# Turned tiles of w_up begun and landed by a table of steps, in place, with a second place for the tile turned last

## The chip, the cores and the metric

The kernel runs on one core of a Trainium2 chip. The metric is the time of one execution on the device in microseconds (us); lower is better. Five engines work side by side, each through its own queue in order: TensorE (PE in the profile, with its weight loads as PEld), VectorE (DVE), ScalarE (ACT), GpSimd (POOL) and SyncE (SP). Here POOL and SP do little but issue transfers (DMAs).

## The reference

One decoder layer for 256 tokens of width 2048, all in float32: a mixer (a state-space group and an attention group side by side) and then a feed-forward part. The change touches the feed-forward part only:

```python
def squared_relu_mlp(u, w_up, w_down):
    hdn = jax.nn.relu(jnp.einsum('bsd,df->bsf', u, w_up))
    return jnp.einsum('bsf,fd->bsd', hdn * hdn, w_down)

h = h + rmsnorm(squared_relu_mlp(rmsnorm(h, norm_mlp_pre), w_up, w_down), norm_mlp_post)
```

`w_up` is 2048 x 8192 and `w_down` 8192 x 2048.

## The kernel before

**Products.** TensorE multiplies numbers of reduced precision, so each float32 operand is split into a high and a low part: `split` (L145) writes `hi` on ACT (L148) and `lo = src - hi` on DVE (L149). A product is three matmuls, `hi*hi`, `hi*lo` and `lo*hi`. Weights come from DRAM in pieces of 256 rows by 512 columns (`raw`, or other buffers that are free at that time), issued on SP; each is split into one of five `hi`/`lo` pairs.

**Units.** A unit (`unit`, L488) makes two neighbouring blocks of 512 output columns for both halves of the tokens (`t` = 0, 1). It goes through `order`, a list of pieces of 256 rows of the weight. At each *step* of it (the loop from L494; steps are counted from 0) it multiplies either in the plain way (`row_tiles`, 24 matmuls with two pieces) or by Strassen's seven products in place of eight (`seven`, 21 matmuls), which needs sums of weights on DVE (L263) and one piece that GpSimd has added up in DRAM. The sevens go into four banks of their own (`more`). After the last of them `combine_new` (L459) brings these banks together into four tiles in SBUF: L464 on ACT, L465 to L468 on DVE, in this order. The last pieces (`last`) are then multiplied plainly, and at each result `at_end` adds the combined part. The next unit uses `acc` and `more` with their places changed, so it begins to write a bank only when `combine_new` has read it.

A w_up unit has seven steps (sevens at steps 1, 3, 4 and 6) and one last piece. The stages after the mixer are: a first pair of w_up blocks made in another way; w_up units for blocks 2, 4 and 6 of the first half; two w_down units; w_up units for blocks 0, 2, 4 and 6 of the second half; two w_down units. The first w_down unit of each half has 14 steps.

**Turned tiles.** A w_up unit ends with four tiles of tokens by features (128 x 512): block 0 with `t` = 0 and 1, then block 1 with `t` = 0 and 1, here called the first to the fourth. They lie in `room["shared"]`: two in `hb`, two in `wpost`. Before w_down can use one, it must be squared, turned to features by tokens, and split. `up_end` (L1486) queues this as `turned` (L1495), a generator in two parts:

- *Begin* (`pump_beside`, L338): Relu with a scale (L1500), Square (L1501), a copy that sorts the upper and lower 16-bit words of the tile into one of two `halves` (L1502), and a transposing DMA on SP from `halves` back into the tile (L1503).
- *Land* (`land_beside`, L347): a copy that puts the words together into `junk` (L1506), and the split into `sh`/`sl` or the `att` tiles (L1508, recorded as L148 and L149).

The tiles of one unit are turned during the next one. A tile is begun at the head of each step from step 2 on. A tile is landed at the end of a step when the oldest one has seen more than two such ends. Before `combine_new`, `drain_beside` (L357) lands whatever is left, because `combine_new` writes the same four tiles. So the first tile is landed at the end of step 4, the second of step 5, and in a w_up unit the third and the fourth at the end of step 6, right before `combine_new`. `hp.tile(..., name="junk")` has one buffer.

**Order.** A planner puts the instructions of each engine in order ahead of time, by its own estimate of when each is ready. Instructions inside `tc.high_priority` (the splits of weights, `combine_new`, the sums at a unit's end) go first; the turned tiles have normal priority, and `tc.issue_after(newest["act"].ins)` keeps each part behind the last split of weights issued on ACT until then. Waits between engines follow from which tile is read and written: a write of a buffer waits for all reads of what was in it.

Of the kernel before, what the change touches and what calls it, by code (L numbers as in the profile page):

```python
# [10 lines left out]
F32 = mybir.dt.float32  # L11
F32R = mybir.dt.float32r
BF16 = mybir.dt.bfloat16
U16 = mybir.dt.uint16
AF = mybir.ActivationFunctionType
ALU = mybir.AluOpType

P = 128
# [21 lines left out]
NB = 512  # L40
# [14 lines left out]
V_SEVENS = (1, 3, 5, 6)  # L55
QK_SEVENS = (1, 3, 5, 6)
PAIRS_AHEAD = 4


def constants():  # L60
# [18 lines left out]
def hymba_layer(ctx: ExitStack, tc: tile.TileContext, x, norm_mix_pre, w_in, conv_w, conv_b, dt_bias, a_log,  # L79
                d_skip, ssm_norm_w, w_out, norm_mix_post, norm_mlp_pre, w_up, w_down, norm_mlp_post,  # L80
                consts, out):
    nc = tc.nc
# [31 lines left out]
    def part(k):  # L114
        if k < NK:
            return sh, sl, k
        i, r = divmod(k - NK, NK // 2)
        return (*att[i], r)
# [26 lines left out]
    def split(hi, lo, src, scale=None):  # L145

        if scale is None:
            return (nc.scalar.activation(hi, src, AF.Copy),  # L148
                    nc.vector.tensor_tensor(lo, src, hi.bitcast(F32), op=ALU.subtract))  # L149
        return (nc.scalar.activation(hi, src, AF.Copy, scale=scale),  # L150
                nc.vector.scalar_tensor_tensor(lo, src, scale, hi.bitcast(F32), op0=ALU.mult, op1=ALU.subtract))
# [27 lines left out]
    room = {}  # L179
# [13 lines left out]
    def beside_up(raws, turn, halves=None):  # L193

        room["sums"] = [v[:, k:k + KB] for k in range(0, NK // 2, KB) for v in att[1]]
        b = hp.tile([P, NT, NB], F32, name="hb")
        room["shared"] = [[b[:, t] for t in range(NT)],
                          [hp.tile([P, NB], F32, name="wpost", bufs=2) for _ in range(NT)]]
        a = hp.tile([P, 3 * KB, NB], F32, name="ha")
        in_a = [a[:, k:k + KB] for k in range(0, 3 * KB, KB)]  # L200
        halves = in_a.pop(0) if halves is None else halves
        room["halves"] = deque(halves[:, i].bitcast(U16) for i in range(KB))
        room["raw"], room["turn"], room["acts"], room["chain"] = [*raws, *in_a], turn, act_u, True
        room["of_halves"], room["of_a"] = halves, in_a
        sums_of.clear()
# [67 lines left out]
    def blocks_of(n):  # L273
        return n if isinstance(n, tuple) else (n * NB, (n + 1) * NB)
# [19 lines left out]
    paired = []  # L294
    places = [dram.tile([P, NB], F32, name=f"pair{i}") for i in range(PAIRS_AHEAD + 1)]

# [35 lines left out]
    def drain():  # L332
        while waiting:
            pump()

    beside, flying = deque(), deque()

    def pump_beside():  # L338

        if not beside:  # L340
            return
        work = beside.popleft()
        with tc.issue_after(newest["act"].ins):
            next(work)
        flying.append([work, 0])

    def land_beside(steps=2):  # L347

        for one in flying:
            one[1] += 1  # L350
        if flying and flying[0][1] > steps:
            with tc.issue_after(newest["act"].ins):
                next(flying.popleft()[0], None)
        if not (beside or flying) and "then" in room:
            room.pop("then")()

    def drain_beside():  # L357
        while beside or flying:
            pump_beside()
            land_beside(0)  # L360

    def row_tile(dst, t, parts, k0, acts, begin, end, cs=slice(0, NB)):

# [124 lines left out]
    def unit(src, n, order, last, acc, more, combine, lag=0, at_end=(None, None), first=True, ending=None,  # L488
             ready=None, halves=None):


        cols = blocks_of(n)
        sevens = [k for k, by_seven in order if by_seven]
        for i, (k, by_seven) in enumerate(order):  # L494
            if i >= 2:
                pump_beside()
            if i + 1 < len(order) and order[i + 1][1]:
                sums_of_acts(order[i + 1][0])
            if by_seven:
                if k == sevens[0]:  # L500
                    drain()
                    if ready:
                        ready()
                seven(src, *cols, k, acc, more, k == sevens[0], k == sevens[-1])
            else:
                for b in range(2):
                    row_tiles(src, cols[b], [k], acc[b::2], room["acts"], first and i == 0, False,
                              fetch=fetch_next)
            land_beside()
            if k == sevens[-1]:  # L510
                drain_beside()
                combine(more)
        for b in range(2):
            if b and ending:
                ended.append(ending(cols[b], last, acc))
            else:
                row_tiles(src, cols[b], last, acc[b::2], room["acts"], False, True, lag if b else 0, at_end[b],
                          fetch=fetch_last if b else fetch_next, halves=halves if b else None)
# [185 lines left out]
    def steps():  # L704
# [5 lines left out]
        with tc.high_priority(offset=AHEAD):  # L710
            for _ in range(PAIRS_AHEAD):
                next_pair()
# [614 lines left out]
    hp = ctx.enter_context(tc.tile_pool(name="hp", bufs=1, reuse_waits="tile"))  # L1327
# [167 lines left out]
    def turned(t, k, r):  # L1495
        room["halves"].rotate(1)
        halves = room["halves"][0]
        ts = slice(t * P, (t + 1) * P)
        words = r.bitcast(U16)
        nc.scalar.activation(r, r, AF.Relu, scale=rmlp[:, t:t + 1])  # L1500
        nc.scalar.activation(r, r, AF.Square)  # L1501
        nc.scalar.activation(halves.rearrange("p (h n) -> p h n", h=2), words.rearrange("p (n h) -> p h n", h=2), AF.Copy)  # L1502
        nc.sync.dma_start_transpose(words.rearrange("p (n s) -> p n s", s=P), halves)  # L1503
        yield
        whole = hp.tile([P, NB], F32, name="junk")
        nc.scalar.activation(whole.bitcast(U16).rearrange("p (n h) -> p h n", h=2), words.rearrange("p (h n) -> p h n", h=2), AF.Copy)  # L1506
        d_h, d_l, i = part(k)
        split(d_h[:, i:i + 4, ts], d_l[:, i:i + 4, ts], whole.rearrange("p (f s) -> p f s", f=4))  # L1508

    def onto_new_mw(more):  # L1510

# [14 lines left out]
    for hf in range(2):  # L1526
        if hf:
            beside_up([], 0)
        for fb in range(0 if hf else 2, 8, 2):
            unit(w_ups[hf], fb, orders[("up", hf), fb], (7,), acc, more,  # L1530
                 lambda x: combine_new(room["shared"], x), 0, (up_end(fb, 0), up_end(fb + 1, 1)))
            acc, more = more, acc
        if hf == 0:
            beside_down()
            unit(w_down, 0, orders[("down", 0), 0], (14, 15), acc, more,
                 lambda x: combine_new(in_mw(0), x), 0, (onto(0), onto(1)))
            room["raw"], room["turn"] = [new_mw(2)], 0
            room["sums"] += room["sums"][:4]
            unit(w_down, 2, orders[("down", 0), 2], (12, 14, 15), more, acc,
                 onto_new_mw, 0, (onto(2), onto(3)))  # L1540
# [65 lines left out]
```

## Time and profile before

| what | value |
|---|---|
| median of 3 runs | 1448.54 us (1445.23 to 1449.48) |
| the profiled execution | 1448.34 us |
| span of its trace | 1446.6 us |
| mean granted clock of TensorE | 0.999 of full speed |
| moved by DMA | 340.31 MB, mean 235 GB/s |

A view of waits lists who waited for what: total us, how many times, longest. A timeline row gives start, duration, engine, line, operation and the tiles as `written<-read`, with the idle time before it and what ended it in brackets. `L149` is line 149 of the kernel; a helper's line stands for all its callers, and the tile names tell them apart (`lo<-raw,hi` is a weight, `sl<-junk,sh` or `al<-junk,ah` a turned tile). The busy time of TensorE counts pipelined matmuls as they overlap: one lasts 0.39 us in the trace while the next starts 0.23 us after it.

### The profile page before, as it was taken

How to read it: one execution, taken by the hardware profiler on the slowest of the kernel's cores; microseconds unless marked ns; L12 is line 12 of the kernel's file. 1: busy time of each engine (PE TensorE's matmuls, PEld its weight loads, DVE VectorE, ACT ScalarE, POOL GpSimd, SP SyncE). 2: the span in 40 equal slices, each digit the busy share in tenths (PEclk: the TensorE clock that was granted, in tenths of full speed). 3: DMA queues.
4: the chain of work that ended last, by engine and by line, in shares of the span. 5: the costliest groups of instructions: out<-in, count | busy, mean ns of one | idle time of the engine just before them, and what ended most of it. 6: DMA issues, size and time to landing. Idle time of an engine off the chain costs nothing. (4 is left out here: it accounts for less than half of the span.)

```text
span 1446.6 us, 20277 instructions
## 1 busy us (share of the span) xinstructions
PE 1432.3 (99%) x6930; PEld 1201.5 (83%) x6930; DVE 1297.6 (90%) x1881; ACT 1000.4 (69%) x1407; POOL 162.6 (11%) x244
## 2 busy tenths in 40 slices
PE   9999999999999999999999999999999999999998
PEld 8888888888888888888888888878888878877886
DVE  7788888988999778689988999999889989989998
ACT  7577669666666666556667668986565689987664
POOL 0201110131111000011100011011111111111000
PEclk9999999999999999999999999999999999999999
DMA  8977656756888648588976799798888999999864
GB/s 268 273 217 225 190 175 186 236 175 195 232 245 255 192 126 251 168 268 261 275 235 213 203 340 288 197 266 244 257 254 262 253 268 288 247 280 293 264 197 150
DMA packets 201927, 340.31 MB, mean 235 GB/s; under 512 B 45616, under 2 KB 48544, under 8 KB 201824
## 3 DMA queue, kind: packets, MB, share of 16 engines
q1 hardware_dynamic: 174304, 279.72, 62.0%
q0 software_dynamic: 19648, 45.63, 15.5%
q10 hardware_dynamic: 7872, 13.68, 2.8%
q8 instruction: 54, 0.88, 0.3%
q14 instruction: 49, 0.40, 0.1%
HBM read 327.39 MB, written 49.84 MB: 261 GB/s over the span
## 5 line engine op out<-in xcount | busy, mean ns | idle before, releaser
L149 DVE TENSOR_TENSOR lo<-raw,hi 128x1024 fp32r<-128x1024 f32 (+1 forms) x390 | 472.6, 1217 | 82.8 <-ACT hi L148 80.6
L148 ACT ACTIVATE hi<-raw 128x1024 fp32r<-128x1024 f32 (+1 forms) x390 | 406.2, 1048 | 170.2 <-PE acc L370 49.1
L526 PE MATMUL acc<-ua,hi 128*128 128x512 f32 x520 | 141.2, 400 | 0.1
L148 ACT ACTIVATE hi<-e 128x1024 fp32r<-128x1024 f32 x66 | 69.7, 1057 | 53.8 <-DVE e L263 50.2
L526 PEld LDWEIGHTS acc<-ua,hi 128*128 128x128 f32 x520 | 91.2, 189 | 14.2 <-ACT hi L148 0.2
L368 PE MATMUL acc<-hi,ua 128*128 128x512 f32 x228 | 90.4, 396 | 0.4 <-DVE wpost L468 0.4
L368 PE MATMUL acc<-hi,sh 128*128 128x512 f32 x220 | 86.6, 394 | 3.0 <-DVE wpost L468 3.0
L369 PE MATMUL acc<-lo,ua 128*128 128x512 f32 x228 | 89.2, 391 | 0.0
L370 PE MATMUL acc<-hi,ua 128*128 128x512 f32 x228 | 89.1, 391 | 0.0
L149 DVE TENSOR_TENSOR lo<-e,hi 128x1024 fp32r<-128x1024 f32 x66 | 80.4, 1218 | 6.4 <-ACT hi L148 6.2
L370 PE MATMUL acc<-hi,sl 128*128 128x512 f32 x220 | 85.7, 390 | 0.0
L369 PE MATMUL acc<-lo,sh 128*128 128x512 f32 x220 | 85.6, 389 | 0.0
L529 PEld LDWEIGHTS acc<-ua,lo 128*128 128x128 f32 x520 | 76.5, 189 | 8.9
L529 PE MATMUL acc<-ua,lo 128*128 128x256 f32 x520 | 78.8, 281 | 0.0
L456 PE MATMUL acc<-lo,ah 128*128 128x512 f32 x180 | 70.6, 392 | 0.7 <-DVE lo L149 0.7
L457 PE MATMUL acc<-hi,al 128*128 128x512 f32 x180 | 70.1, 389 | 0.0
L455 PE MATMUL acc<-hi,ah 128*128 128x512 f32 x180 | 70.1, 389 | 0.0
L526 PE MATMUL acc<-uc,hi 128*128 128x512 f32 x208 | 61.4, 405 | 0.0
L149 DVE TENSOR_TENSOR lo<-ha,hi 128x1024 fp32r<-128x1024 f32 x48 | 58.3, 1218 | 3.0 <-ACT hi L148 2.7
L148 ACT ACTIVATE hi<-ha 128x1024 fp32r<-128x1024 f32 x48 | 50.2, 1050 | 6.9 <-PE acc L370 2.0
L456 PE MATMUL acc<-lo,ua 128*128 128x512 f32 x137 | 53.4, 390 | 0.2 <-DVE lo L149 0.2
L455 PE MATMUL acc<-hi,ua 128*128 128x512 f32 x137 | 53.5, 391 | 0.0
(565 smaller groups left out, 3717.0 us busy)
## 6 DMA issues: line engine op xcount, KB each, us to landing
raw<-in_w_in_dram SPq DMA_DIRECT2D x154, 512.0 KB, 4.4
raw<-in_w_down_dram SPq DMA_DIRECT2D x70, 512.0 KB, 5.7
raw<-in_w_up_dram SPq DMA_DIRECT2D x65, 512.0 KB, 5.0
raw<-in_w_out_dram SPq DMA_DIRECT2D x38, 512.0 KB, 5.2
raw<-pair SPq DMA_DIRECT2D x59, 256.0 KB, 4.7
pair<-in_w_up_dram POOLq DMA_DIRECT2D x56, 256.0 KB, 5.8
pair<-in_w_down_dram POOLq DMA_DIRECT2D x52, 256.0 KB, 5.9
ha<-in_w_up_dram SPq DMA_DIRECT2D x25, 512.0 KB, 6.8
```

The source lines that it names most:

```text
L148: return (nc.scalar.activation(hi, src, AF.Copy), nc.vector.tensor_tensor(lo, src, hi.bitcast(F32), op=ALU.subtract))
L149: nc.vector.tensor_tensor(lo, src, hi.bitcast(F32), op=ALU.subtract))
L368: nc.tensor.matmul(dst[:, cs], a_h[:, r, ts], hi[:, j, cs], start=begin and j == 0, stop=False)
L369: nc.tensor.matmul(dst[:, cs], a_h[:, r, ts], lo[:, j, cs], start=False, stop=False)
L370: product[t] = nc.tensor.matmul(dst[:, cs], a_l[:, r, ts], hi[:, j, cs], start=False, stop=end and j == KB - 1)
L455: nc.tensor.matmul(dst, a_h, hi[:, j], start=own and first, stop=False)
L456: nc.tensor.matmul(dst, a_h, lo[:, j], start=False, stop=False)
L457: nc.tensor.matmul(dst, a_l, hi[:, j], start=False, stop=own and last)
L526: nc.tensor.matmul(acc[f], hi[:, j, f * P:(f + 1) * P], u(k0 + j), start=k0 + j == 0, stop=False, skip_group_check=True)
L529: nc.tensor.matmul(acc[f][:, 0], lo[:, j, f * P:(f + 1) * P], u(k0 + j)[:, 0], start=False, stop=k0 + j == NK - 1, skip_group_check=True)
```

## The change

Tiles are begun at steps 1, 2, 4 and 5 (`TURNS`) in place of steps 2, 3, 4 and 5. They are landed at the ends of steps listed in `LANDS`: 0, 3, 4 and 6 in a unit of up to seven steps, and 0, 3, 4, 6 and 7 in a longer one. The count of ends that a tile has seen is gone. The first, second and third tile of a unit land at steps 3, 4 and 6 of the next unit, and the fourth at step 0 of the unit after that, or at step 7 where the next unit is the first one of w_down. The call of `drain_beside` before `combine_new` is gone.

Because the fourth tile is now still in use when the next `combine_new` writes, it has two places, one in `wpost` and one in `junk`, which units take in turn (`room["last"]`). The words are put together in the `halves` that they came from, not in `junk`; so a tile's half is in use from L1502 until its split on DVE, and the two halves still go in turn.

```diff
+TURNS = (1, 2, 4, 5)
+LANDS = ((0, 3, 4, 6), (0, 3, 4, 6, 7))
...
         room["shared"] = [[b[:, t] for t in range(NT)],
                           [hp.tile([P, NB], F32, name="wpost", bufs=2) for _ in range(NT)]]
+        room["last"] = deque([room["shared"][1].pop(), hp.tile([P, NB], F32, name="junk")])
+        room["shared"][1].append(room["last"][0])
...
         with tc.issue_after(newest["act"].ins):
             next(work)
-        flying.append([work, 0])
-
-    def land_beside(steps=2):
-
-        for one in flying:
-            one[1] += 1
-        if flying and flying[0][1] > steps:
+        flying.append(work)
+
+    def land_beside():
+
+        if flying:
             with tc.issue_after(newest["act"].ins):
-                next(flying.popleft()[0], None)
+                next(flying.popleft(), None)
...
-            land_beside(0)
+            land_beside()
...
         for i, (k, by_seven) in enumerate(order):
-            if i >= 2:
+            if i in TURNS:
                 pump_beside()
...
-            land_beside()
+            if i in LANDS[len(order) > 7]:
+                land_beside()
             if k == sevens[-1]:
-                drain_beside()
                 combine(more)
...
-        whole = hp.tile([P, NB], F32, name="junk")
-        nc.scalar.activation(whole.bitcast(U16).rearrange("p (n h) -> p h n", h=2), words.rearrange("p (h n) -> p h n", h=2), AF.Copy)
+        nc.scalar.activation(halves.rearrange("p (n h) -> p h n", h=2), words.rearrange("p (h n) -> p h n", h=2), AF.Copy)
         d_h, d_l, i = part(k)
-        split(d_h[:, i:i + 4, ts], d_l[:, i:i + 4, ts], whole.rearrange("p (f s) -> p f s", f=4))
+        split(d_h[:, i:i + 4, ts], d_l[:, i:i + 4, ts], halves.bitcast(F32).rearrange("p (f s) -> p f s", f=4))
...
         for fb in range(0 if hf else 2, 8, 2):
+            room["last"].rotate(1)
+            room["shared"][1][1] = room["last"][0]
             unit(w_ups[hf], fb, orders[("up", hf), fb], (7,), acc, more,
```

## The prediction

> **What bounds the kernel now.** I read the page first, for the busy shares.
>
> ```profile
> span 1446.6 us, 20277 instructions
> PE 1432.3 (99%) x6930; PEld 1201.5 (83%) x6930; DVE 1297.6 (90%) x1881; ACT 1000.4 (69%) x1407; POOL 162.6 (11%) x244
> ```
>
> TensorE is idle for 1446.6 - 1432.3 = 14.3 us of the span. Nothing in the change takes a matmul away, so only idle time of TensorE can be won, and only where the changed code runs. That is from the first w_up unit with turned tiles to the first steps of the last w_down unit, 820 to 1330 us of the span. Next I read the waits in that window: TensorE's (PE), its weight loads' (PEld), ScalarE's (ACT) and VectorE's (DVE). Columns: total us, times, longest.
>
> ```profile
> PE acc L368 <- DVE wpost L468: 3.4, 3, 2.0
> PE ps L369 <- DVE lo L149: 1.2, 2, 0.7
> PE acc L456 <- DVE lo L149: 0.9, 2, 0.7
> PEld acc L368 <- DVE wpost L468: 5.5, 5, 2.4
> PEld acc L456 <- DVE lo L149: 3.0, 6, 1.1
> PEld ps L369 <- DVE lo L149: 2.1, 2, 1.1
> ACT junk L1506 <- DVE sl L149: 10.1, 3, 3.4
> ACT junk L1506 <- DVE al L149: 3.0, 4, 1.1
> ACT ha L1502 <- DMA hb<-ha: 5.1, 2, 2.6
> DVE lo L149 <- ACT hi L148: 25.9, 40, 2.7
> ```
>
> TensorE's idle time here is 3.4 + 1.2 + 0.9 = 5.5 us, and 5 + 6 + 2 = 13 weight loads were late. A late one costs more than its idle time, as TensorE's timeline shows at one restart:
>
> ```profile
> 943.42 0.50 PE L368 MATMUL acc<-hi,sh 128*128 128x512 f32 x1 [1.05 <-DVE wpost L468]
> 943.76 0.39 PE L369 MATMUL acc<-lo,sh 128*128 128x512 f32 x1
> 943.99 0.40 PE L370 MATMUL acc<-hi,sl 128*128 128x512 f32 x1
> ```
>
> The matmul after the wait takes 0.34 us to the next one's start, and the next 0.23: 0.11 us more for each restart. 13 x 0.11 = 1.4, so about 5.5 + 1.4 = **6.9 us** can be won at most.
>
> The largest item is the wait for L468, the last operation of `combine_new`, at the end of a unit. The chain of waits says where it comes from:
>
> ```profile
> 940.63 0.61 DVE al L149
> 941.27 1.38 ACT junk L1506
> 942.67 0.70 DVE wpost L468
> ```
>
> L468 writes the place of the fourth turned tile. That place is free only when L1506 has landed the fourth tile of the unit before, and L1506 writes the single `junk` buffer, which is free only after the third tile's split on DVE (al, L149). TensorE's next unit adds into the bank that L468 reads, so it stands. This is the entry into the first w_down stage. At the entry into the second it is the same chain:
>
> ```profile
> 1273.34 1.33 ACT L1506 ACTIVATE junk<-wpost 128x1024 uint16<-128x1024 uint16 x1
> 1274.81 0.68 DVE L468 TENSOR_TENSOR wpost<-acc,wpost 128x512 f32<-128x512 f32 x1
> 1275.55 0.50 PE L368 MATMUL acc<-hi,sh 128*128 128x512 f32 x1 [1.99 <-DVE wpost L468]
> ```
>
> **The change, part by part.** The work of one turned tile stays as it is:
>
> ```profile
> L1500 ACT ACTIVATE hb<-hb,rmlp x14: 702/708/712, 858.3 to 1276.5; 128x512 f32<-128x512 f32 x14
> L1501 ACT ACTIVATE wpost<-wpost x14: 615/633/637, 869.0 to 1298.7; 128x512 f32<-128x512 f32 x14
> L1502 ACT ACTIVATE ha<-wpost x8: 1040/1058/1059, 1162.5 to 1299.3; 128x1024 uint16<-128x1024 uint16 x8
> L1506 ACT ACTIVATE junk<-hb x14: 1340/1370/1392, 874.7 to 1301.2; 128x1024 uint16<-128x1024 uint16 x14
> L148 ACT ACTIVATE sh<-junk x12: 613/616/630, 877.8 to 1231.9; 128x512 fp32r<-128x512 f32 x12
> L149 DVE TENSOR_TENSOR sl<-junk,sh x12: 681/683/693, 879.9 to 1238.9; 128x512 fp32r<-128x512 f32 x12
> DMA to landing us min/median/max: 2.7/6.8/10.3
> ```
>
> Beginning a tile is 0.71 + 0.63 + 1.06 = 2.40 us of ACT and one transposing DMA on SP; landing it is 1.37 + 0.62 = 1.99 us of ACT and 0.68 us of DVE. The 28 tiles keep their counts. Writing `halves` in place of `junk` (same shape and type) I take at 1.37 us again, so at nothing. Only order and waits change.
>
> *Second place for the fourth tile.* It lands after step 0 of the next unit, and L468 writes the other place, so L468 no longer waits for L1506. Term A, the two entries into w_down: 1.05 + 1.99 idle and 2 x 0.11, together 3.26 us. I keep all of it, if the copies behind are early enough. They are:
>
> ```profile
> 941.36 1.21 DVE L149 TENSOR_TENSOR lo<-raw,hi 128x1024 fp32r<-128x1024 f32 x1
> 950.81 0.39 PE L369 MATMUL acc<-lo,sh 128*128 128x512 f32 x1
> ```
>
> This lo is ready at 942.57 and used at 950.81, 8.2 us later. Term B, between w_up units: 3.4 - 1.05 - 1.99 = 0.36 idle, with the other 5 - 2 = 3 restarts 0.33: 0.69 us. There almost nothing lies behind the stall:
>
> ```profile
> 1191.38 1.21 DVE L149 TENSOR_TENSOR lo<-e,hi 128x1024 fp32r<-128x1024 f32 x1
> 1192.81 0.39 PE L456 MATMUL acc<-lo,ah 128*128 128x512 f32 x1
> ```
>
> Ready at 1192.59, used at 1192.81: a TensorE that comes 0.65 us earlier waits here instead. B lies between 0 and 0.69; I take half, 0.35.
>
> *First tile begun at step 1, halves used in place, `junk` buffer gone.* Term C is what is left: 1.2 + 0.9 = 2.1 us idle and 13 - 5 = 8 restarts, 0.9: 3.0 us. Its largest pieces come from L1502 of a third tile, which waits until the first tile's transpose has read the same half:
>
> ```profile
> 1162.55 1.06 ACT L1502 ACTIVATE ha<-wpost 128x1024 uint16<-128x1024 uint16 x1 [2.54 <-DMA hb<-ha]
> 1164.59 1.23 DVE L149 TENSOR_TENSOR lo<-e,hi 128x1024 fp32r<-128x1024 f32 x1 [2.72 <-ACT hi L148]
> 1165.87 0.50 PE L456 MATMUL acc<-lo,ah 128*128 128x512 f32 x1 [0.69 <-DVE lo L149]
> ```
>
> ACT stood 2.54 us, DVE 2.72 behind it, TensorE 0.69. The wait row above has two such waits, 5.1 us together. With the change the first tile begins a step earlier and the third still at step 4, so the transpose has one more step (about 5 us of matmuls: 24 x 0.23). The room for this on ACT is there:
>
> ```profile
> 855.89 1.06 ACT L148 ACTIVATE hi<-e 128x1024 fp32r<-128x1024 f32 x1 [6.24 <-DVE e L263]
> ```
>
> ACT stood 6.24 us before step 1's copies while the first tile's 2.40 us lay behind them (L1500's row above starts at 858.3). Of C, between 0 and 3.0, I take 2.0: both DMA waits gone, the small ones half left. SP is moved past too: a transpose issued earlier stands ahead of weight loads that it followed. I price that at nothing while loads come before ACT needs them; if that cover goes, a load is later by one issue of L1503, 1.2 to 4.9 us by its own row:
>
> ```profile
> L1503 SPq DMA_TRANSPOSE hb<-ha x8: 1231/2080/4917, 1153.1 to 1287.3; - x8
> ```
>
> *The wait that is added.* L1502 of a tile now also waits for the DVE split of the tile two before it in the same half. For the third and fourth tiles that split was issued just before, at the end of steps 3 and 4. Behind the waiting L1502 in ACT's queue stand the hi copies of the next step, DVE's lo behind them, and TensorE behind those. No row shows this wait. The nearest is L1506 waiting for the same kind of split: 3.0 us in 4, 0.75 each, up to 3.4. Below, it is 0: Relu and Square come first, 1.34 us, longer than a split of 0.68. Cover is the ACT idle time of a unit, 41.40 - 37.81 = 3.59 us in the second row of the windows here (length, then busy PE, PEld, DVE, ACT, POOL, clock, DMA):
>
> ```profile
> 851.30:897.90 46.60, 46.60 (x207) 38.61 (x206) 43.76 (x53) 37.53 (x45) 6.79 (x10) 1.00 1.04 302
> ...
> 1189.70:1231.10 41.40, 41.35 (x181) 33.61 (x181) 40.34 (x49) 37.81 (x46) 5.44 (x8) 1.00 1.03 279
> ```
>
> Seven units carry tiles (28 / 4). Term D lies between 0 and 7 x 2.6 = 18.2 us (one wait a unit, as long as L1502's longest). I take one unit of seven uncovered at 0.75, the nearest row.
>
> **Sum.** 3.26 + 0.35 + 2.0 - 0.75 = 4.86 us. The profiled execution took 1448.34 us, 1.7 more than its span and 0.2 less than the median 1448.54: 1448.34 - 4.86 = **1443.5 us**.
>
> **The rivals.** *VectorE is the bound inside the w_up units.* For it: DVE is idle in the second window for only 41.40 - 40.34 = 1.06 us, and TensorE's uses follow lo by 0.2 us. Against it: in the first window TensorE has no idle time at all with the same DVE work per step, and DVE waits for ACT 25.9 us in all. If it holds, B and C give nothing and A stays: 1448.34 - 3.26 + 0.75 = 1445.8 us. The Trainium skill, page Perfetto Trace Analysis, section Identifying the Most-Contended Engine, speaks for it: matmul busy time is no measure for TensorE, the share of LDWEIGHTS is, and the engine with the highest occupancy is the one to relieve. By that, DVE with 90% stands above TensorE with 83%, and the sum would be this rival's. The trace agrees with the 0.2 us and not with the first window, so it does not decide.
>
> *The change doesn't do what it says.* L467 still writes the third tile's place, and that tile lands after step 6, right ahead of `combine_new`. If its L1506 is late, L467 and L468 behind it are late as before, and with A and B gone the time is 1448.34 - 2.0 + 0.75 = 1447.1 us. Against it: that L1506 no longer waits for a split.
>
> *The added wait isn't covered (slower).* The place is L1502 of the third tile at step 4, between two steps done by seven products, where DVE is full. It decides from the point where the wait, less ACT's spare time there, passes 0.8 us in each of the seven units (7 x 0.8 = 5.6, all that A, B and C give). At L1502's longest, 2.6 us: 1448.34 - 5.61 + 18.2 = 1460.9 us; at 1.5 us, 1453.2. For it: the 2.54 us at 1162.55 went through to TensorE. Against it: L1506's waits for a split, 13.1 us of ACT, stand beside losses of TensorE of 6.9 us from all causes, so more than half of such waits is covered now. The Trainium skill, Perfetto Trace Analysis, section Tensor Engine Instruction, calls the queues of ACT and DVE strictly first in, first out, so nothing passes a waiting L1502; the three rows around 1162.55 agree.
>
> **How the numbers follow.** About 0.3%, 4.3 us, is what a measurement of this kernel can tell from no change; that puts the edge at 1444.2. The forecast, A with most of C, 1441.4 to 1444.2: 0.52. VectorE as bound, 1444.2 to 1446.5: 0.30. No effect, 1446.5 to 1448.8: 0.08. Added wait uncovered: 0.10, and nearly all of it beyond 1450. Faster 0.52, same 0.38, slower 0.10. The range goes from 1440.5 (all 6.9 us won, and 0.9 for a median of few runs that spread from 1445.23 to 1449.48) to 1450.0; the uncovered wait's upper part stays out.
>
> **What would show it.** In the changed profile: no wait of TensorE for L468 at the two entries into w_down (A right); L1502's waits for a transpose gone (C right); no wait of L1502 for a split above 0.8 us (D right); DVE idle of about 1 us in a w_up unit while TensorE still waits for lo (the first rival). The prediction is wrong if TensorE waits for L467 in place of L468, if ACT waits at L1506 for a transpose, or if more than 6.9 us go, which would have to come from outside this window.

## The result, and the profile after

| | before | after |
|---|---|---|
| median, beside each other on one chip | 1449.48 us (1445.23 to 1451.11, 7 runs) | 1459.23 us (1454.35 to 1461.19, 7 runs) |
| the profiled execution | 1448.34 us | 1457.27 us |
| span of its trace | 1446.6 us | 1455.5 us |

The ratio is 1.0066, with a 95% interval from 1.0048 to 1.0084: **slower by 0.7%**, where 1443.5 us and faster had been forecast. The diff moves the lines: L1500 to L1503 and L1506 of before are L1502 to L1505 and L1507 here, L148 and L149 are L150 and L151, L468 is L470, L368 to L370 are L370 to L372, and L456 is L458.

The page's first lines of the changed kernel:

```profile
span 1455.5 us, 20245 instructions
PE 1436.1 (99%) x6930; PEld 1205.0 (83%) x6930; DVE 1296.8 (89%) x1881; ACT 1000.4 (69%) x1407; POOL 162.3 (11%) x244
```

The span is 8.9 us longer. TensorE's idle time went from 14.3 to 1455.5 - 1436.1 = 19.4 us, 5.1 more. The other 3.8 us are busy time: the same 6930 matmuls took longer, to which I come below.

The view by windows of the changed kernel, for two stretches of w_up units (columns as in the prediction):

```profile
850.00:927.00 77.00, 77.00 (x341) 63.76 (x340) 74.05 (x90) 68.28 (x81) 10.29 (x15) 1.00 1.04 285
1120.00:1262.00 142.00, 142.00 (x627) 117.39 (x626) 137.56 (x166) 121.65 (x144) 18.43 (x27) 1.00 0.97 268
```

In 219 us of w_up units TensorE is never idle. The wait for the last operation of `combine_new` is gone, and so are all others there. Every wait that TensorE still has lies in the first w_down unit of each half. These are all of TensorE's waits, and ScalarE's that bear on them, between 820 and 1345 us:

```profile
PE ps L370 <- ACT hi L150: 7.2, 4, 3.4
PE ps L371 <- DVE lo L151: 2.8, 4, 0.8
PE acc L458 <- DVE lo L151: 0.7, 1, 0.7
ACT ha L1504 <- DVE sl L151: 4.3, 2, 3.1
ACT ha L1504 <- DVE al L151: 2.6, 1, 2.6
ACT mw L1504 <- DVE al L151: 0.5, 1, 0.5
ACT ha L1507 <- DMA hb<-ha: 4.7, 2, 3.7
ACT mw L1507 <- DMA junk<-mw: 3.2, 1, 3.2
ACT mw L1507 <- DMA hb<-mw: 3.0, 1, 3.0
ACT ha L1507 <- DMA wpost<-ha: 1.5, 1, 1.5
```

They sum to 10.7 us for TensorE, where before showed 5.5. The last four rows are new: a landing (L1507) that waits for its own transpose, 12.4 us in all.

**Where it went.** I number TensorE's matmuls, take the time from the start of one to the start of a later one, and subtract 0.2267 us for each in between. That is the spacing of matmuls 4400 to 4850 in the changed kernel, where TensorE never stands (142.00 us / 627 in the row above gives 0.2265; by that no entry changes by more than 0.2). What is left is time lost, in the same work whatever the kernel:

| loss, us | w_up units, up to their end | first w_down unit, first half | first w_down unit, second half |
|---|---|---|---|
| matmuls | 4400-4850, 5650-6230 | 4850-5650 | 6230-6900 |
| before | 1.8 + 5.1 | 0.0 | 2.6 |
| after | 0.0 + 0.2 | 8.2 | 9.7 |

The w_up columns end behind the waits for L468 in the kernel before, at 943.42 and 1275.55, and so hold them. The last column runs on into the second w_down unit.

So 6.7 us were won, more than the 5.61 that A, B and C were taken at, and 15.3 were lost elsewhere: 8.6 in all, of the 8.9.

**How it is lost.** The last tiles of the w_up unit before and the first of the new unit meet at the entry into w_down. From ScalarE's timeline of the changed kernel (the ah rows are ScalarE's part of the split of a landed tile; an `x2` joins two operations):

```profile
929.42 0.61 ACT L150 ACTIVATE ah<-mw 128x512 fp32r<-128x512 f32 x1
...
935.66 1.32 ACT L1502 ACTIVATE hb<-hb,rmlp 128x512 f32<-128x512 f32 x2
936.88 0.61 ACT L1503 ACTIVATE hb<-hb 128x512 f32<-128x512 f32 x1
...
951.10 1.06 ACT L1504 ACTIVATE mw<-hb 128x1024 uint16<-128x1024 uint16 x1 [0.53 <-DVE al L151]
...
960.11 1.37 ACT L1507 ACTIVATE mw<-hb 128x1024 uint16<-128x1024 uint16 x1 [2.98 <-DMA hb<-mw]
...
970.95 0.61 ACT L150 ACTIVATE ah<-mw 128x512 fp32r<-128x512 f32 x1
...
973.41 1.04 ACT L1504 ACTIVATE mw<-junk 128x1024 uint16<-128x1024 uint16 x1
...
980.02 1.34 ACT L1507 ACTIVATE mw<-junk 128x1024 uint16<-128x1024 uint16 x1 [3.15 <-DMA junk<-mw]
981.24 2.92 ACT L150 ACTIVATE hi<-raw 128x1024 fp32r<-128x1024 f32 x3
```

and from VectorE's and TensorE's:

```profile
950.38 0.69 DVE L151 TENSOR_TENSOR al<-mw,ah 128x512 fp32r<-128x512 f32 x1
...
971.95 0.69 DVE L151 TENSOR_TENSOR al<-mw,ah 128x512 fp32r<-128x512 f32 x1
...
982.30 1.23 DVE L151 TENSOR_TENSOR lo<-raw,hi 128x1024 fp32r<-128x1024 f32 x1 [2.71 <-ACT hi L150]
```

```profile
982.32 0.49 PE L370 MATMUL ps<-hi,sh 128*128 128x512 f32 x1 [2.10 <-ACT hi L150]
983.58 0.50 PE L371 MATMUL ps<-lo,sh 128*128 128x512 f32 x1 [0.77 <-DVE lo L151]
983.92 0.40 PE L372 MATMUL ps<-hi,sl 128*128 128x512 f32 x1
984.15 0.52 PE L370 MATMUL ps<-hi,sh 128*128 128x512 f32 x1
984.47 0.63 PE L371 MATMUL ps<-lo,sh 128*128 128x512 f32 x1
984.90 0.63 PE L372 MATMUL ps<-hi,sl 128*128 128x512 f32 x1
```

The half that the new unit's first tile needs held a tile of the unit before. ScalarE wrote that tile's `ah` at 929.42; VectorE's half of the same split came at 950.38, 21 us later, behind weight copies and sums. Until then the tile kept its half. The first tile was squared at 937.49, but its word sort L1504 ran at 951.10. Of these 13.6 us only 0.53 are shown as a wait: the planner had put L1504 that late in ScalarE's queue. Its transpose therefore flew late, and the landing, fixed to the end of step 3, stood 2.98 us for it. The fourth tile had to wait for its half too, though here the hold was mostly ScalarE's own: the second tile, landed at 964.89, got its `ah` only at 970.95 and VectorE's half 1.0 us later, so the fourth, squared at 966.73, was sorted at 973.41. Its landing at 980.02 stood 3.15 us with three weight splits behind it in the queue; VectorE stood 2.71 us behind those and TensorE 2.10 and 0.77. In the second half stands of the same kind give TensorE a wait of 3.4 us, the longest in the list above.

In the kernel before, the two halves of the split at this entry lie 7 us apart:

```profile
933.53 0.61 ACT L148 ACTIVATE ah<-junk 128x512 fp32r<-128x512 f32 x1
...
940.56 0.68 DVE L149 TENSOR_TENSOR al<-junk,ah 128x512 fp32r<-128x512 f32 x1
```

**And a slower clock.** In TensorE's last rows above a matmul takes 0.63 us, and the next one starts 0.43 us after it in place of 0.23. By windows of the changed kernel:

```profile
984.10:987.50 3.40, 3.40 (x10) 2.60 (x10) 3.02 (x5) 1.10 (x3) 0.81 (x1) 0.52 0.65 196
1309.60:1315.00 5.40, 4.86 (x11) 3.52 (x12) 4.88 (x7) 4.33 (x6) 0.81 (x1) 0.50 0.72 123
```

The granted clock is 0.52 and 0.50 there. TensorE is busy 3.40 us for 10 matmuls and 4.86 for 11, where 21 take 21 x 0.2267 = 4.76: 3.5 us more, which is nearly all of the 3.8 us of longer busy time.

### The profile page after: what moved, and what is told of

Its sections match the earlier page's. It is cut to its first block, busy times and chain, and to the rows that moved or that the text cites. A ratio compares the mean times of both kernels' runs of the same rounds, so it can differ in the third digit from the quotient of the medians.

```text
span 1455.5 us, 20245 instructions
## 1 busy us (share of the span) xinstructions
PE 1436.1 (99%) x6930; PEld 1205.0 (83%) x6930; DVE 1296.8 (89%) x1881; ACT 1000.4 (69%) x1407; POOL 162.3 (11%) x244
## 4 chain that ended last, share of the span: by engine, by line
PE 65%; ACT 4%; DVE 3%; DMA 3%; issue 2%; ACTq 0%; SPq 0%; DVEq 0%
PE acc L371 9%; PE acc L372 9%; PE acc L370 9%; PE acc L458 6%; PE acc L459 6%; PE acc L457 6%; PE acc L528 4%; PE ps L371 3%; PE ps L372 2%; PE ps L370 2%; ACT hi L150 2%; PE acc L531 2%; PE ps L457 2%; PE ps L459 2%; PE ps L458 2%
## 5 line engine op out<-in xcount | busy, mean ns | idle before, releaser
L151 DVE TENSOR_TENSOR lo<-raw,hi 128x1024 fp32r<-128x1024 f32 (+1 forms) x390 | 473.4, 1219 | 82.6 <-ACT hi L150 79.8
L150 ACT ACTIVATE hi<-raw 128x1024 fp32r<-128x1024 f32 (+1 forms) x390 | 406.2, 1049 | 174.7 <-PE acc L372 52.8
L150 ACT ACTIVATE hi<-e 128x1024 fp32r<-128x1024 f32 x66 | 69.9, 1058 | 54.9 <-DVE e L267 49.9
L370 PE MATMUL acc<-hi,ua 128*128 128x512 f32 x228 | 90.0, 395 | 0.0
L372 PE MATMUL acc<-hi,ua 128*128 128x512 f32 x228 | 89.0, 390 | 0.0
L370 PE MATMUL acc<-hi,sh 128*128 128x512 f32 x220 | 86.4, 393 | 0.0
L151 DVE TENSOR_TENSOR lo<-e,hi 128x1024 fp32r<-128x1024 f32 x66 | 80.5, 1220 | 5.8 <-ACT hi L150 5.7
L372 PE MATMUL acc<-hi,sl 128*128 128x512 f32 x220 | 85.7, 390 | 0.0
L458 PE MATMUL acc<-lo,ah 128*128 128x512 f32 x180 | 70.1, 390 | 0.0
L151 DVE TENSOR_TENSOR lo<-ha,hi 128x1024 fp32r<-128x1024 f32 x48 | 58.4, 1221 | 4.8 <-ACT hi L150 4.8
L150 ACT ACTIVATE hi<-ha 128x1024 fp32r<-128x1024 f32 x48 | 50.3, 1050 | 8.0 <-issue 2.9
L458 PE MATMUL acc<-lo,ua 128*128 128x512 f32 x137 | 53.3, 389 | 0.0
```

Of the source, the lines that this page charges most:

```text
L150: return (nc.scalar.activation(hi, src, AF.Copy), nc.vector.tensor_tensor(lo, src, hi.bitcast(F32), op=ALU.subtract))
L370: nc.tensor.matmul(dst[:, cs], a_h[:, r, ts], hi[:, j, cs], start=begin and j == 0, stop=False)
L372: product[t] = nc.tensor.matmul(dst[:, cs], a_l[:, r, ts], hi[:, j, cs], start=False, stop=end and j == KB - 1)
L458: nc.tensor.matmul(dst, a_h, lo[:, j], start=False, stop=False)
```

## The experiments

Loss as in the table above; time and ratio against the kernel before, run beside it. Theory H is the chain just told: the half that is held until a late split. Theory S blames the landing steps as such. The forecasts count the second half's entry by other stretches, from matmul 6200 to 6400 and so with the wait for L468: 4.9 us in the kernel before, 6.4 with the words apart, 7.3 with both cures.

| run | median, us | ratio, 95% interval | w_up | first half | second half |
|---|---|---|---|---|---|
| split first | 1451.06 | 1.0015 [1.0006, 1.0024] | 1.8 | 0.4 | 7.3 |
| land one later | 1465.46 | 1.0118 [1.0101, 1.0135] | 0.8 | 6.6 | 19.0 |
| old steps in w_down | 1465.04 | 1.0118 [1.0103, 1.0133] | 0.2 | 5.4 | 18.5 |
| in place only | 1472.22 | 1.0167 [1.0152, 1.0182] | 19.0 | 3.3 | 11.6 |
| split first, old steps | 1456.06 | 1.0054 [1.0039, 1.0070] | 2.1 | 3.8 | 10.5 |
| words apart | 1452.60 | 1.0022 [1.0012, 1.0032] | 0.2 | 3.6 | 8.0 |
| apart, split first, old steps | 1450.00 | 1.0006 [0.9996, 1.0017] | 2.3 | 0.4 | 8.6 |
| apart, old steps | 1454.84 | 1.0034 [1.0021, 1.0048] | 0.2 | 4.9 | 10.0 |
| apart, split first | 1450.26 | 1.0006 [0.9995, 1.0017] | 2.2 | 0.6 | 7.8 |
| the same, transposes on ScalarE | 1450.90 | 1.0012 [0.9998, 1.0025] | 3.5 | 2.3 | 5.1 |
| the same, second half only | 1449.37 | 1.0005 [0.9993, 1.0017] | 1.8 | 1.0 | 6.3 |
| the same, one of two there | 1457.49 | 1.0051 [1.0035, 1.0067] | 4.3 | 1.2 | 13.6 |

**Split first.** VectorE's half of a turned tile's split goes among the urgent instructions, so the half is free sooner:

```diff
-        split(d_h[:, i:i + 4, ts], d_l[:, i:i + 4, ts], halves.bitcast(F32).rearrange("p (f s) -> p f s", f=4))
+        whole = halves.bitcast(F32).rearrange("p (f s) -> p f s", f=4)
+        nc.scalar.activation(d_h[:, i:i + 4, ts], whole, AF.Copy)
+        with tc.high_priority(offset=AHEAD):
+            nc.vector.tensor_tensor(d_l[:, i:i + 4, ts], whole, d_h[:, i:i + 4, ts].bitcast(F32), op=ALU.subtract)
```

> The changed kernel with one thing more: the DVE part of a turned tile's split gets the priority of the weights' splits. Theory H (the half is held until that split, which has normal priority and came 21 us after ACT's part in the first w_down unit; so tiles begin late and their landings stand for the transposes): L1504 of the first tile in the first w_down unit within 5 us of its Relu, L1507's waits for a transpose (12.3 us in the changed kernel) below 3 us, no TensorE wait above 1 us there, time 1440 to 1446 us. Theory S (the table's steps 3 and 4 are too early in that unit, whatever the split): L1507's waits stay above 8 us, time 1454 to 1461.

The time is 8.2 us below that of the changed kernel, and the loss in the first half's entry fell from 8.2 to 0.4. Its timelines of VectorE and ScalarE (L1510 and L1512 are the two halves of the split here):

```profile
940.03 0.68 DVE L1512 TENSOR_TENSOR al<-mw,ah 128x512 fp32r<-128x512 f32 x1
```

```profile
935.91 0.63 ACT L1510 ACTIVATE ah<-mw 128x512 fp32r<-128x512 f32 x1
...
940.10 1.04 ACT L1504 ACTIVATE mw<-hb 128x1024 uint16<-128x1024 uint16 x1
...
952.31 1.36 ACT L1507 ACTIVATE mw<-hb 128x1024 uint16<-128x1024 uint16 x1
```

The split is done 4.1 us after its `ah`, not 21; the first tile is sorted at 940.10, not 951.10; the landing waits for nothing. H holds there. But the forecast of a gain on the kernel before missed, because the second half's entry still loses 7.3 us, and landings still wait 3.8 us for transposes there, where under 3 us had been forecast.

**Land one later**, and **old steps in w_down**: in the long units the landings move from steps 3 and 4 to 4 and 5, in the second run the begins too, to the steps of before:

```diff
-LANDS = ((0, 3, 4, 6), (0, 3, 4, 6, 7))
+LANDS = ((0, 3, 4, 6), (0, 4, 5, 6, 7))
...
-            if i in TURNS:
+            if i in (TURNS if len(order) <= 7 else (2, 3, 4, 5)):
```

(the first run has the first edit alone)

> The changed kernel, landings of a long unit at 0, 4, 5, 6, 7 in place of 0, 3, 4, 6, 7. S: the waits of L1507 go, 1441 to 1447 us. H: tiles still begin late, but the landings stand less; 1447 to 1455, with L1507's waits at 3 to 8 us.

> The changed kernel, but in long units tiles begin at steps 2, 3, 4, 5 and land at 0, 4, 5, 6, 7, as in the kernel before but for the fourth tile of the unit before it. S: 1441 to 1447 us. H: the first tile still begins late because its half is held, so no better than the version that only lands one step later, within 2 us of it.

Both are 6 us slower than the changed kernel and 0.4 us apart. That is as H has it for the second run; for the first run the times of both theories are missed. The landings' waits for a transpose do fall, from 12.4 us to 2.2 and 1.8, and yet the time rises. In the run with the landings alone moved, ScalarE's word sorts (L1504) now wait as well, until the transpose of the tile that had the half before has read it:

```profile
PE ps L370 <- ACT hi L150: 12.7, 4, 6.0
ACT ha L1504 <- DMA hb<-ha: 5.3, 2, 4.7
ACT mw L1504 <- DMA hb<-mw: 4.4, 2, 2.3
```

These two runs change more than a step, so they do not settle S by themselves: the first tile now lands behind the sort of the third, which uses the same half, and in place its landing must then also wait for the third tile's transpose. "Words apart" against "apart, old steps", further down, is the cleaner pair, since the tiles begun in the w_down units there leave their half when they land. With the later steps the entries lose 4.9 and 10.0 us, with the earlier ones 3.6 and 8.0. S falls by that.

**In place only.** The kernel before with one part of the change: the words put together in `halves`; `junk` is not used. Steps and the drain stay as before.

```diff
-        whole = hp.tile([P, NB], F32, name="junk")
-        nc.scalar.activation(whole.bitcast(U16).rearrange("p (n h) -> p h n", h=2), words.rearrange("p (h n) -> p h n", h=2), AF.Copy)
+        nc.scalar.activation(halves.rearrange("p (n h) -> p h n", h=2), words.rearrange("p (h n) -> p h n", h=2), AF.Copy)
...
-        split(d_h[:, i:i + 4, ts], d_l[:, i:i + 4, ts], whole.rearrange("p (f s) -> p f s", f=4))
+        split(d_h[:, i:i + 4, ts], d_l[:, i:i + 4, ts], halves.bitcast(F32).rearrange("p (f s) -> p f s", f=4))
```

> The kernel before with one part of the change: the words are put together in the halves, the steps and the drain ahead of the combination stay. H: begins wait for splits, so the third and fourth tile of each unit come later and the waits for L468 grow: 1453 to 1465 us. S: 1447 to 1451, as before.

It is 22.9 us slower, more than either theory had. Its waits (the lines are those of the kernel before up to L1503; the landing is L1505), with one landing:

```profile
ACT ha L1502 <- DMA hb<-ha: 8.7, 5, 3.3
ACT mw L1502 <- DMA hb<-mw: 6.3, 4, 2.7
PE acc L368 <- DVE wpost L468: 6.1, 4, 2.3
```

```profile
881.63 1.37 ACT L1505 ACTIVATE mw<-hb 128x1024 uint16<-128x1024 uint16 x1 [2.16 <-DMA wpost<-mw]
```

And of the kernel before, the row that the prediction's list leaves out:

```profile
ACT mw L1502 <- DMA hb<-mw: 0.8, 1, 0.8
```

With the steps of before, L1502 waits 15.0 us for transposes (5.1 + 0.8 before) and the wait for L468 grows from 3.4 to 6.1. The landing shown at 881.63 says why, and it is not only the late split of H: with the old steps a first tile lands after the third has been sorted into the same half, so in place its landing waits for the third tile's transpose (`wpost<-mw`). Nine landings of first and second tiles wait like this, 8.0 us in all. The in-place words are thus the costly part of the change, and its new steps and second place pay for them in the w_up units: 19.0 us lost there without these, 0.2 with them.

**Split first, old steps**: the edits of "split first" and "old steps in w_down" together, to see whether the earlier begins are what hurts in the second half.

> The version with the DVE split first, and in long units the steps of before (begin 2, 3, 4, 5; land 0, 4, 5, 6, 7). Its sister without these steps still lost 7 us at the entry into the second w_down unit, where a transpose stood on SP ahead of weight loads (SP waited 5.2 us for ACT, then ACT 4.6 us for a load). Theory Q (SP's order is the second cause): the begin one step later puts the loads first; ACT's waits for weight loads from 820 us on fall from 13.3 to under 6 us, time 1443 to 1447. If landing late is itself the cost (it was without the priority: 1465), 1450 to 1460.

They are not: 5.0 us slower than with the split first alone, within the range of the rival that landing late is the cost. (The landings in place behind the third tile's sort come back with these steps.) ScalarE's waits for w_down tiles were to fall from 13.3 us to under 6, and they grow:

```profile
ACT hi L150 <- DMA raw<-in_w_down_dram: 20.8, 13, 5.9
```

**Words apart.** The changed kernel, but in the w_down units the words are put together in that one of the two places of the fourth tile that is free; the half is free at once when they are:

```diff
+        room["apart"] = len(order) > 7
...
-        nc.scalar.activation(halves.rearrange("p (n h) -> p h n", h=2), words.rearrange("p (h n) -> p h n", h=2), AF.Copy)
+        whole = room["last"][1] if room.get("apart") and r is not room["last"][1] else halves.bitcast(F32)
+        nc.scalar.activation(whole.bitcast(U16).rearrange("p (n h) -> p h n", h=2), words.rearrange("p (h n) -> p h n", h=2), AF.Copy)
...
-        split(d_h[:, i:i + 4, ts], d_l[:, i:i + 4, ts], halves.bitcast(F32).rearrange("p (f s) -> p f s", f=4))
+        split(d_h[:, i:i + 4, ts], d_l[:, i:i + 4, ts], whole.rearrange("p (f s) -> p f s", f=4))
```

> The changed kernel, normal priority, but in the w_down units the words of a landed tile are put together in the free one of the two places of the fourth tile, so that a half is free when L1507 has begun from it, not when DVE has split. Theory H (hold of the half): the begins of the third and fourth tile no longer wait, but the first and second still wait for the splits of the w_up unit before: half of the loss back, 1450 to 1456 us. If the hold is no cause: 1457 to 1461.

6.6 us of the loss come back without any urgency: H again, from the other side. The first tile still waits for the tile that was landed in place in the w_up unit (its sort runs at 951.51), which fits the 3.6 us that stay there.

**Combinations.** Words apart with the old steps, with and without the urgent split, and with the new steps and the urgent split:

> All three: DVE split first, old steps in long units, words put together apart from the halves there. H and Q together: no TensorE wait above 1 us after 820 us, 1441 to 1445 us, faster than the kernel before. If ACT's or DVE's load in these units is the bound instead: within 2 us of the version without the apart place.

> The changed kernel with two things undone in the w_down units alone: the words are put together in a place of their own (as in the run with the words apart), and the tiles begin and land at the steps of before (begun at 2, 3, 4, 5, landed at 0, 4, 5, 6, 7), the split in its ordinary order. What is left of the change is all in the w_up units, and the two entries without the wait of L468. Theory O (the second entry's loss, 6.4 us with the words apart against 4.9 us before, comes of the earlier begins, whose transposes stand in SP's queue ahead of the w_down loads): the second entry loses 2 to 3 us, the first 0 to 2, the stretches of w_up stay near 0, and the time is 1444 to 1447. Rival C (the entry is bound by the w_down loads and the VectorE work itself, whatever the steps; the wait of L468 in the kernel before only stood for part of it): the second entry loses 6 to 10 us as in the four runs with other steps, and the time is 1450 to 1453.

> The changed kernel at its own steps, with both cures at once: the words put together apart in the w_down units, and the VectorE part of the turned tile's split in the higher priority. Theory H (both act on the same held place of halves: either one alone gave back 6.6 to 8 us of the 9.8 us, so the two don't add): 1450 to 1452.5, the first entry under 1 us, the second 6 to 8 us, ACT's waits for the w_down loads 6 to 14 us in all. Rival A (they cure different entries, the priority the first and the place the second, and add): 1444 to 1448, the second entry under 4 us.

The first run is faster than the one without the apart place by 6.1 us, but not faster than the kernel before, and misses both of its forecasts. The two cures don't add (1450.26 against 1451.06 and 1452.60), as H has it: both act on the same half. The old steps bring nothing in the second half (10.0 against 8.0 with the words apart), so theory O falls; rival C had the size of that entry's loss, but its time, 1450 to 1453, is missed too. The best of these are level with the kernel before and not faster, since what w_up gives (4.7 us of 6.9 in the last run) goes into the second half's entry.

**Transposes on ScalarE.** What is late at that entry? SP's timeline of the run "apart, split first" (L1505 is the word sort there, L1506 the transpose):

```profile
1256.73 9.91 SPq L164 DMA_DIRECT2D raw<-in_w_down_dram  x4
1271.48 1.24 SPq L1506 DMA_TRANSPOSE hb<-ha  x1
1272.82 1.05 SPq L164 DMA_DIRECT2D raw<-in_w_down_dram  x2
```

and ScalarE's:

```profile
1270.42 1.04 ACT L1505 ACTIVATE ha<-hb 128x1024 uint16<-128x1024 uint16 x1
...
1272.98 1.05 ACT L150 ACTIVATE hi<-raw 128x1024 fp32r<-128x1024 f32 x1
1278.60 1.06 ACT L150 ACTIVATE hi<-raw 128x1024 fp32r<-128x1024 f32 x1 [4.58 <-DMA raw<-in_w_down_dram]
```

SP issues nothing for 4.8 us, its transpose waiting for ScalarE's sort, which ends at 1271.46, with two loads behind it that ScalarE wants soon after. So the transposes of the w_down units were moved to ScalarE's queue:

```diff
-        nc.sync.dma_start_transpose(words.rearrange("p (n s) -> p n s", s=P), halves)
+        (nc.scalar if room.get("apart") else nc.sync).dma_start_transpose(words.rearrange("p (n s) -> p n s", s=P), halves)
```

In the second run this holds in the second half alone, in the third there for the first and third tile alone:

```diff
-        (nc.scalar if room.get("apart") else nc.sync)
+        (nc.scalar if room.get("apart") and room.get("half") else nc.sync)
...
+        room["half"] = hf
...
-        (nc.scalar if room.get("apart") and room.get("half") else nc.sync)
+        (nc.scalar if room.get("apart") and room.get("half") and not t else nc.sync)
```

> The run with both cures (words apart, priority, steps of the changed kernel; 1450.3, second entry 7.3 us), with one edit more: in the w_down units the DMA transposes of the turned tiles are issued by ScalarE's queue instead of SP's, so that no w_down load stands behind a transpose that waits for its halves. Theory Q (at the second entry ScalarE's 4.6 us wait for a w_down tile comes of that: SP issued nothing from 1266.6 to 1271.5, the transpose waiting for ScalarE's word sort, with two loads behind it): ACT's waits for the w_down loads between 1255 and 1320 fall under 3 us, none over 2 us, the second entry loses 2 to 5 us, and the time is 1446 to 1449 (the four issues cost ScalarE 1.2 us or more each, beside idle time of it). Rival V (the loads are only late in the profile because their places come free late, and VectorE's work ends last anyway): the second entry still loses 6 to 9 us and the time is 1450 to 1453.

> The run with ScalarE issuing the transposes (1450.9), but only in the second half's w_down unit; the first half's stay on SP, where they cost 0.6 + 0.6 us and not 2.4 + 2.3. Theory Q (each queue hurts at one entry: SP's at the second, where loads stand behind it, ScalarE's at the first, where its copies do): the first entry's stretches lose 1 to 2 us in all, the second 4 to 5, and the time is 1447 to 1449. Rival V (what is won in one stretch comes back in a later one): 1450 to 1452.

> As the run before it, but in the second half's w_down unit ScalarE issues only the transposes of the first and third tile; the second and fourth are SP's again, placed there behind the loads. What goes is the issue that held ScalarE for 4.64 us (the second transpose, right behind the first). Theory Q: the second entry loses 2 to 4 us and the time is 1445 to 1447.5, level with the kernel before or up to 0.3% faster. Rival V: the second entry still loses 4.5 to 7 us, since VectorE's sums and lo copies end last there whatever the transposes do, and the time is 1448 to 1451.

In the first of the three ScalarE's waits for w_down loads are gone there (none of 0.3 us or more), and that entry loses 5.1 us in place of 7.8, as theory Q has it (4.7 as the forecasts count). The time, 1450.90, is not in Q's range but in the rival's. ScalarE pays for the issues, as its timeline shows:

```profile
1277.76 4.64 ACTq L1506 DMA_TRANSPOSE hb<-ha  x1
1282.50 2.01 ACT L150 ACTIVATE hi<-raw 128x1024 fp32r<-128x1024 f32 x2 [3.82 <-issue]
```

One issue held it for 4.64 us, and the first half's entry got worse. The rival's reason, that VectorE's work ends last there, is not what this run shows: between 1276 and 1296 us VectorE is busy for 13.90 of 20.00 us and stands 3.30 and 3.32 us for ScalarE's `hi`, which come behind the begins of two turned tiles and behind that issue. With the second half alone the time is level with before (1.0005), a bit above the range that theory Q gave, as is the second entry's loss. The third run missed both forecasts: the second entry lost 13.6 us. SP's waits there, between 1270 and 1312 us:

```profile
SPq L1506 <- DMA wpost<-ha: 10.2, 1, 10.2
SPq L159 <- DMA hb<-ha: 8.8, 1, 8.8
```

SP's transpose stood 10.2 us until the one that ScalarE had issued for the third tile had landed. ScalarE then stood 8.27 us at the landing that needed SP's transpose, and TensorE 8.1.

## Why the prediction was wrong, point by point

- **A, the waits for L468: right as to the waits**, none is left; but the copies behind the stall were shown to be early at the first entry alone. There the time stays won once the split is urgent (0.4 us lost behind it). At the second entry every run without the wait loses at least 5.1 us from matmul 6200 on, where the kernel before loses 4.9 with it (2.3 of them at that wait). That A's part there is lost again a few steps on fits this, but is not shown.
- **B, and C inside w_up: right**, and rather low: the three terms were taken at 5.61 us, and w_up with its ends gave 6.7. The most that could be won, 6.9 us, was put too low: by the starts of matmuls the kernel before loses 1.8 + 5.1 + 2.6 = 9.5 us in the same stretches. But of C's 2.1 us of idle time 1.4 lay in the second half's w_down unit, and there nothing was won: L1502's waits for a transpose are gone, and waits for splits and for landings stand in their place.
- **The first rival, VectorE as the bound inside the w_up units: wrong.** VectorE is busy for 137.56 of 142.00 us there, and TensorE for all of them. Its waits were a matter of order. The rule that the prediction draws from the Trainium skill, page Perfetto Trace Analysis, section Identifying the Most-Contended Engine, by which VectorE was the engine to relieve, does not fit this stage.
- **The second rival, the third tile's late landing: wrong.** TensorE waits for no operation of `combine_new`.
- **D, the added wait: here the prediction failed**, in place and in size. I took 0.75 us, once, in a w_up unit; the change lost 15.3 us in the two w_down units (with the slower clock, below). Three steps of its working failed:
  - "That split was issued just before": the split has two halves on two engines. ScalarE's was issued, and VectorE's ran 21 us later. It held back the new unit's first tile, by 13.6 us, where the prediction looked at the third and fourth only. In the kernel before VectorE's half came 7 us after ScalarE's, and there the urgent L468 hung on it through `junk` and L1506; with a second place for the fourth tile nothing urgent does. The urgent split brought 4.1 us, which agrees; that the planner's order came from just this was not tried by itself.
  - The bounds, 0 to 18.2 us, were made from waits. Waits of L1504 for a split are 4.3 + 2.6 + 0.5 us in the list after, and they hide the larger part: 13.6 us of delay stand as 0.53 us of wait, since the planner moves the instruction and fills the gap. What a held buffer costs is read from how late the instruction runs.
  - The cover, ScalarE's idle time in a w_up unit, was there: no w_up unit lost anything. The price fell due at the entry into w_down, which was not priced at all.
- **The third rival, slower by the added wait, was right in its sign and in the kind of its cause**, a sort that waits for a split; it named the third tile at step 4 of the w_up units, where nothing was lost, and had 0.10. That its times, 1453.2 to 1460.9, hold the measured one is luck: they are seven waits in w_up units, none of which cost anything. Its reason against, that more than half of such waits were covered, was read from waits in the kernel before that no fixed landing step stood behind.
- **"Wrong if ACT waits at L1506 for a transpose"**: that is what happened (L1507 now, 4.7 + 3.2 + 3.0 + 1.5 us). I had named it and given it no price. That nothing passes a waiting instruction in ScalarE's queue, as the Trainium skill, page Perfetto Trace Analysis, section Tensor Engine Instruction, has it, agrees with the three weight splits behind the landing at 980.02.
- **SP's price**, 1.2 to 4.9 us if loads lose their cover, was set at nothing. After H was cured it came due: ScalarE waits 4.58 us for a load behind a transpose.
- **The clock** was no term of the sum: 3.5 us of the loss.

What stays open is the second half's entry: the runs nearest to the kernel before lose 5.1 to 8.6 us there, where that kernel loses 2.6, or 4.9 with its wait for L468. Loads behind transposes are a part of it, 2.7 us by the run with ScalarE's queue. No version here beats the kernel before; the closest, at 1449.37 us, is no different from it.

## What to carry to other kernels

A change that lets a buffer be held longer is priced at its last release, on whichever engine that runs and at whatever priority, and at every stage that the buffer reaches, also the one after the stage that is being mended. In a kernel whose order is planned, a delay can show as a later start and hardly as a wait: compare when the instruction's inputs were ready with when it ran. And a wait that is taken away may have been what made the planner put something early; look for what loses its urgency with it, above all where later steps are fixed by a table.

## What the hardware showed that I had not expected

In this case TensorE's granted clock halved after short idle times and stayed so for some microseconds: at 984.1 for 3.4 us, after idle pieces of 2.10 and 0.77 us with one matmul between them, and at 1309.6 for 5.4 us, after a piece of 3.4 us. A single piece of 1.99 us, in the kernel before at 1275.55, had no such effect: the matmul after it took 0.50 us and the next ones 0.39 again. Nor had pieces of 1.62 and 0.76 us in the run with the words apart (a granted clock of 1.00 from 1306 to 1310). The Trainium skill, page TensorE: Matmul & The Clock Gate, Part 1, gives a half clock after at least one idle window of about 3.4 us; the second place agrees, while at the first the idle time was 2.9 us and not in one piece. These stands of TensorE cost about half as much again: 3.5 us for 2.10 + 0.77 + 3.4 us.

In the run "the same, one of two there" SP's queue stood until a transpose issued by ScalarE had landed: 10.2 us at SP's own next transpose, and 8.8 us at a load. The Trainium skill, page DMA: Bandwidth & Descriptors, section Silent corruption: two transposing streams in flight at once, asks that transposes of two queues wait for each other; the 10.2 us are what such a wait cost here, though no run shows what put it there. The load that stood writes a part of `ha`, the tile from which the halves are cut, so that it may have waited for a buffer; this is not shown either.
